# Mixer B's value products: eight matmuls of a step in one row instead of two rows of four

## The chip, the cores and the metric

The kernel runs on one core of a Trainium2 chip. The time is device microseconds of one execution of the whole program. Three runs of the kernel before gave 2955.64, 2964.18 and 2974.54 us. TensorE (PE) does the matmuls and the transposes, VectorE (DVE), ScalarE (ACT) and GpSimd (POOL) the rest; transfers are issued from SyncE (SP). PEld stands for TensorE's weight loads, which have rows of their own in the profile.

## The reference, cut to what matters

One step of a two-layer decoder for a prompt of 2048 tokens and a group of 8 samples. The even layer has two branches, A (a gated MLP) and B (stick-breaking attention with 8 heads of 64 channels); the odd layer has C (sparse attention over selected keys) and D (pooling). The change lies in B for the prompt:

```python
def stick_breaking(q, k, v, q_pos, k_pos):
    z = einsum('bqhd,bkhd->bhqk', q, k) * HEAD_DIM ** -0.5
    mask = k_pos[None, :] < q_pos[:, None]
    log_keep = where(mask, log_sigmoid(-z), 0.0)
    later = cumsum(log_keep, axis=3, reverse=True) - log_keep
    att = where(mask, exp(log_sigmoid(z) + later), 0.0)
    return einsum('bhqk,bkhd->bqhd', att, v)
```

The last line is what the value products compute. The kernel writes it with the running product `P` of the kept shares and with differences of neighbouring value rows in place of the values, so that a sum over key tiles of `P` times a tile of value differences remains.

## The kernel before, in words

The prompt's 2048 tokens are cut into four blocks of 512, and a block into four tiles of 128. `mixer_b(i)` does branch B of block i: for each of four head pairs m and each key block s from i down to 0, two steps, one for head a=0 and one for head a=1. That is 4 x (1+2+3+4) = 40 pairs of steps over the four blocks. In each pair:

- `b_logits` (one call a head): for each of four query tiles two matmuls into `z` (L839), a sigmoid on ACT (L846, or L843 with a DVE operation, L844, where mixer C's stage needs another table), on the diagonal block a mask on POOL (L849), and a scan on DVE (L853) that leaves the running product in the tile `P`.
- `b_values` (one call a head, woven with the logits of the next step): for each of four key tiles kb up to four transposes of `P` on TensorE (L876) and a copy back on ACT (L877). For head a=1 the value products follow (L885): for a key tile k, one matmul a head into the upper or the lower half of the 64-row pair in the PSUM tile `av`. They are full fp32 matmuls of 64 weight columns, and each is two records in the trace.

When s reaches 0, DVE reads `av` into `b_sum` (L892), POOL multiplies by the gate and SP stores it for the output projection.

Instructions are recorded by a Python program of generators. Each `yield` gives a cost, and `par` runs several generators side by side: it always takes the next piece from the stream that has used the smallest share of its declared cost. For mixer B the declared cost is `B(i) = 8 * (3.2 + 1.6 + 4.8 * i)`; the generator's yields come to 3.2 for the logits of two heads, 3.2 for the transposes and 1.6 after each row of value products. The order in which pieces are recorded is also the order in which tiles that share a buffer (PSUM banks above all) get it.

After recording, `Order` plans all five engines anew with a list of costs. In it matmuls on half the array's columns (`halves`) that follow each other on TensorE and write the same tile are tied into a group that stays together; the groups, and everything else, may move among each other. The result is fixed as the order of each engine's queue.

There are three stages, each with its own pools: the first does layer 0's projections and mixer B of blocks 0 to 2 (to about 1300 us in the trace), the second mixer B of block 3 beside mixer C's first tiles and the selection of keys (to about 2050 us), the third the rest of mixer C. L549 to L551 are the projections' matmuls in three parts (`pp`), L944 to L946 the output projection's (`pp_o`), L1581, L1612 and L1626 mixer C's logits, transposes and value products, L567 the samples' share of a projection, L1215 a matmul of branch D.

Of the kernel before, what the change touches and what calls it, by code (L numbers as in the profile page):

```python
# [44 lines left out]
NT = TB // P  # L45
# [393 lines left out]
class Body:  # L439
# [419 lines left out]
    def b_values(self, i, step, st, Ps):  # L859


        nc = self.nc
        m, a, s = step
        diag = s == i
        Ps = st["pT", a] = Ps[0]
        if a == 0:
            vs = st["vs"] = self.b0.tile([P, NT, P], F32, tag="vs", name="vs", bufs=self.bufs["vs"])
            nc.sync.dma_start(vs, self.vsc[s][m])
        if a and diag:
            st["av"] = self.pavb.tile([P, TB], F32, tag="av", name="av")  # L870
        vs = st["vs"]
        for kb in range(NT):
            t0, c = kb if diag else 0, slice(kb * P, (kb + 1) * P)
            pt = self.ps("ps_p", [P, NT, P])
            for t in range(t0, NT):
                nc.tensor.transpose(pt[:, t, :], Ps[:, t, c], self.idf)  # L876
            nc.scalar.copy(Ps[:, t0:, c], pt[:, t0:])  # L877
            yield 0.4
            if a == 0 or kb % 2 == 0:
                continue  # L880
            av = st["av"]
            for k in (kb - 1, kb):
                t0 = k if diag else 0
                for h in range(2):
                    nc.tensor.matmul(av[64 * h:64 * h + 64, t0 * P:], vs[:, k, 64 * h:64 * h + 64],  # L885
                                     st["pT", h][:, t0:, k * P:(k + 1) * P],
                                     start=diag and k == 0, stop=s == 0 and k == NT - 1)
            yield 1.6
        if a and s == 0:
            sm = self.tmp("b_sum")  # L890
            ve = self.vea[i][:, m].unsqueeze(2).broadcast_to([P, NT, P])
            nc.vector.tensor_tensor(sm.rearrange("p (t i) -> p t i", t=NT), st["av"].rearrange("p (t i) -> p t i", t=NT),  # L892
                                    ve, op=OP.add)
            g = self.otile("gb")
            nc.sync.dma_start(g, self.gbd[i][m])
            nc.gpsimd.tensor_tensor(sm, sm, g, op=OP.mult)
            nc.sync.dma_start(self.otd[0][i][4 + m], sm)
# [1398 lines left out]
```

## Time and profile before

| | |
|---|---|
| median of three runs | 2964.18 us |
| the profiled execution's own time | 2964.62 us |
| its span, first to last instruction | 2962.9 us |
| TensorE's granted clock, mean | 0.96 |
| busy: PE, DVE, ACT, POOL | 93%, 73%, 53%, 38% |
| idle in front of PE's z_c, longest group of waits | 27.3 us |

A busy share is an average over stages. A matmul's row gives its start and its modelled length; matmuls are pipelined, so the next one starts before the one ahead has ended, and the spacing of the starts is what a matmul takes of TensorE.

### The profile page before, as it was taken

Reading aid. Unit: us, or ns where it says so; the run is one execution under the profiler, and the core shown is the slowest. Engines: PE = TensorE matmul, PEld = TensorE weight load, DVE = VectorE, ACT = ScalarE, POOL = GpSimd, SP = SyncE. Lnnn points to the kernel's source line nnn. Section 1 sums busy time; section 2 is a strip of 40 time slices with the busy share of each in tenths; the row PEclk is TensorE's granted clock in tenths of the full one; section 3 lists DMA queues with packets and bytes.
Section 4 is the critical chain, followed back from the end, with each engine's and each line's share of the span. In section 5 each row is a group of like instructions: output and inputs, shape, how many; then the busy total and the mean of one; then the engine's idle time right before and its main releaser. Section 6 shows DMA issues by size and latency. Waiting matters only on the chain. (4 is left out here: it accounts for less than half of the span.)

```text
span 2962.9 us, 52295 instructions
## 1 busy us (share of the span) xinstructions
PE 2747.0 (93%) x17490; PEld 2184.8 (74%) x17490; DVE 2163.9 (73%) x5493; ACT 1561.7 (53%) x3148; POOL 1112.2 (38%) x1172
## 2 busy tenths in 40 slices
PE   7998999989999999979799999998899998998995
PEld 6886777767767777768477677777777887887885
DVE  2366557856775887438988998897897778887766
ACT  2433333334444344435466677784577666675852
POOL 2323335423324543242433422335422555344342
PEclk9999999999999999989899999999999999998998
DMA  7566865776585668453665455425655565675452
GB/s 220 166 175 195 266 191 186 239 227 205 172 245 165 216 184 292 147 155 111 194 173 152 140 144 146 122 79 146 189 164 157 171 190 161 213 216 172 129 185 67
DMA packets 536594, 523.51 MB, mean 177 GB/s; under 512 B 43184, under 2 KB 408905, under 8 KB 536288
## 3 DMA queue, kind: packets, MB, share of 16 engines
q1 hardware_dynamic: 526439, 484.29, 55.1%
q0 software_dynamic: 9856, 35.66, 3.9%
q8 instruction: 138, 2.26, 0.3%
q14 instruction: 161, 1.31, 0.1%
HBM read 430.27 MB, written 89.73 MB: 176 GB/s over the span
## 5 line engine op out<-in xcount | busy, mean ns | idle before, releaser
L478 POOL TENSOR_TENSOR wl<-wr,wh 128x512 fp32r<-128x512 f32 x260 | 410.7, 1580 | 967.8 <-ACT wh L475 810.5
L549 PE MATMUL pp<-xh,wh 128*128 128x512 f32 (+1 forms) x1536 | 635.6, 417 | 10.2 <-DVE q_hl L468 6.1
L550 PE MATMUL pp<-xl,wh 128*128 128x512 f32 (+1 forms) x1536 | 616.4, 402 | 9.6 <-DVE rs_t L494 8.2
L551 PE MATMUL pp<-xh,wl 128*128 128x512 f32 (+1 forms) x1536 | 616.0, 401 | 1.0 <-DVE wl L478 1.0
L475 ACT CAST wh<-wr 128x1024 fp32r<-128x1024 f32 x260 | 269.9, 1038 | 386.5 <-PE pp L550 198.7
L478 DVE TENSOR_TENSOR wl<-wr,wh 128x512 fp32r<-128x512 f32 x260 | 219.0, 843 | 210.7 <-ACT wh L475 190.0
L549 PEld LDWEIGHTS pp<-xh,wh 128*128 128x128 f32 (+1 forms) x1536 | 288.6, 189 | 95.7 <-issue 27.8
L550 PEld LDWEIGHTS pp<-xl,wh 128*128 128x128 f32 (+1 forms) x1536 | 290.6, 189 | 68.6 <-issue 9.3
L551 PEld LDWEIGHTS pp<-xh,wl 128*128 128x128 f32 (+1 forms) x1536 | 289.6, 189 | 63.9 <-issue 4.6
L944 PE MATMUL pp_o<-wh,oh 128*128 128x256 f32 x1008 | 301.0, 300 | 17.9 <-ACT oh L462 11.8
L946 PE MATMUL pp_o<-wh,ol 128*128 128x256 f32 x1008 | 291.5, 293 | 2.6 <-POOL ol L468 2.6
L945 PE MATMUL pp_o<-wl,oh 128*128 128x256 f32 x1008 | 293.2, 292 | 0.0
L853 DVE TENSOR_TENSOR_SCAN P<-P,bfst 128x512 f32<-128x512 f32 x192 | 268.5, 1408 | 22.3 <-ACT P L846 21.8
L877 ACT COPY P<-ps_p 128x512 f32<-128x512 f32 (+1 forms) x320 | 166.0, 523 | 189.2 <-PE ps_p L876 180.4
L1581 PE MATMUL z_c<-ksc,qc 128*128 128x512 f32 (+3 forms) x816 | 222.0, 355 | 32.6 <-DVE mx L1583 27.3
L1599 ACT ACTIVATE zt<-zt,nmax 128x512 f32<-128x512 f32 (+3 forms) x320 | 209.0, 655 | 76.8 <-DVE nmax L1587 76.3
L1614 ACT COPY zt<-ps_pc 128x512 f32<-128x512 f32 (+3 forms) x320 | 164.1, 520 | 114.9 <-PE ps_pc L1612 113.3
L944 PEld LDWEIGHTS pp_o<-wh,oh 128*128 128x128 f32 x1008 | 198.1, 197 | 28.7 <-ACT oh L462 13.2
L1568 POOL TENSOR_TENSOR nm<-nm,mk 128x256 f32<-128x256 f32 (+1 forms) x128 | 92.7, 725 | 335.1 <-DMA nm<-bft 186.1
L839 PE MATMUL z<-ks,q 128*128 128x512 f32 (+3 forms) x640 | 194.0, 391 | 18.9 <-DMA ks<-ksc 10.8
L946 PEld LDWEIGHTS pp_o<-wh,ol 128*128 128x128 f32 x1008 | 197.1, 197 | 8.8 <-POOL ol L468 4.5
L945 PEld LDWEIGHTS pp_o<-wl,oh 128*128 128x128 f32 x1008 | 198.5, 197 | 5.2 <-issue 2.1
(456 smaller groups left out, 5861.2 us busy)
## 6 DMA issues: line engine op xcount, KB each, us to landing
pg<-cache_b_kv SPq DMA_DIRECT2D x256, 256.0 KB
wr<-w_in_even SPq DMA_DIRECT2D x112, 512.0 KB
wr<-w_in_odd SPq DMA_DIRECT2D x76, 512.0 KB
wr<-w_out SPq DMA_DIRECT2D x68, 512.0 KB
ks<-ksc SPq DMA_DIRECT2D x80, 256.0 KB
ksc<-kcs SPq DMA_DIRECT2D x80, 256.0 KB
q<-qsc SPq DMA_DIRECT2D x64, 256.0 KB
qc<-qcs SPq DMA_DIRECT2D x128, 128.0 KB
```

The source lines that it names most:

```text
L475: nc.scalar.copy(hi, raw)
L478: e.tensor_tensor(lo[:, c], raw[:, c], hi[:, c].bitcast(F32), op=OP.subtract)
L549: nc.tensor.matmul(ps[:m], wh[:, kt, :m], xh[kt], start=a, stop=False)
L550: nc.tensor.matmul(ps[:m], wh[:, kt, :m], xl[kt], start=False, stop=False)
L551: nc.tensor.matmul(ps[:m], wl[:, kt, :m], xh[kt], start=False, stop=b)
L839: nc.tensor.matmul(z[:, :n], q2[:, c, t * P:(t + 1) * P].bitcast(F32R), ks[:, :n].bitcast(F32R), start=c == 0, stop=c == 1)
L853: nc.vector.tensor_tensor_scan(r, r, r, initial=ini, op0=OP.mult, op1=OP.bypass)
L944: nc.tensor.matmul(ps[:, :256], oh[:, tt], wh[:, k], start=a, stop=False)
L945: nc.tensor.matmul(ps[:, :256], oh[:, tt], wl[:, k], start=False, stop=False)
L946: nc.tensor.matmul(ps[:, :256], ol[:, tt], wh[:, k], start=False, stop=b)
L1581: nc.tensor.matmul(z[:, :n], q2[:, c, jj % 2, :].bitcast(F32R), kk, start=c == 0, stop=c == 1)
L1599: nc.scalar.activation(zt, zt, AF.Exp, bias=nmx, accum_out=st["rs"][:, h, c:c + 1])
```

## The change

In `b_values` the value products no longer follow every second key tile, two key tiles of two heads each; all four key tiles of both heads follow the last one. With the row that is gone goes its `yield 1.6`, so that mixer B's generator gives 8.0 instead of 9.6 for a pair of steps. `B(i)`, by which `par` shares out the stages, is as before. The matmuls themselves, their operands and their order within `av` are the same.

```diff
             yield 0.4
-            if a == 0 or kb % 2 == 0:
+            if a == 0 or kb < NT - 1:
                 continue
             av = st["av"]
-            for k in (kb - 1, kb):
+            for k in range(NT):
                 t0 = k if diag else 0
                 for h in range(2):
                     nc.tensor.matmul(av[64 * h:64 * h + 64, t0 * P:], vs[:, k, 64 * h:64 * h + 64],
                                      st["pT", h][:, t0:, k * P:(k + 1) * P],
```

TensorE's queue before, block 1, head pair 1, the diagonal key block: two rows of value products.

```order
L550 MATMUL pp<-xl,wh 128x512
L885 MATMUL av<-P,vs 64x512 x2
L885 MATMUL av<-P,vs 64x384 x2
L876 MATMUL ps_p<-idf,P 128x128 x2
L839 MATMUL z<-ks,q_6697 128x512
L876 MATMUL ps_p<-idf,P 128x128
L839 MATMUL z<-ks,q_6697 128x512 x3
L551 MATMUL pp<-xh,wl 128x512
L885 MATMUL av<-P,vs 64x256 x2
L885 MATMUL av<-P,vs 64x128 x2
L839 MATMUL z<-ks,q_7261 128x128 x2
```

TensorE's queue after, the same pair of steps:

```order
L551 MATMUL pp<-xh,wl 128x512
L885 MATMUL av<-P,vs 64x512 x2
L885 MATMUL av<-P,vs 64x384 x2
L885 MATMUL av<-P,vs 64x256 x2
L885 MATMUL av<-P,vs 64x128 x2
L876 MATMUL ps_p<-idf,P 128x128 x4
L549 MATMUL pp<-xh,wh 128x512
```

The eight matmuls stand together, and the transposes and logits that stood between them stand outside.

TensorE's queue before, near the end of mixer B of block 3, at the first row of its last pair of steps (the second follows 16 rows below it; `zt` and `ksc` are mixer C's):

```order
L567 MATMUL ps_smp<-wl,xsT 16x128
L885 MATMUL av<-P,vs 64x512 x4
L1612 MATMUL ps_pc<-idf,zt 128x128 x4
L876 MATMUL ps_p<-idf,P 128x128 x4
L1215 MATMUL ps_m<-pl,dwg 128x512
L551 MATMUL pp<-xh,wl 128x512
L1581 MATMUL z_c<-ksc,qc 128x512 x2
```

TensorE's queue after, the same last value products of block 3:

```order
L551 MATMUL pp<-xh,wl 128x512
L885 MATMUL av<-P,vs 64x512 x8
L1271 MATMUL z_i<-kid,qi 128x512
L567 MATMUL ps_smp<-wh,xsT 16x128
L1612 MATMUL ps_pc<-idf,zt 128x128 x4
```

Of the four `ps_m` matmuls of that block three stand ahead of the last value products before (the `ps_m` row above is the third), and none after: all of mixer B of block 3 has moved ahead of them. In PE's queue as a whole, 80 rows of four `av` matmuls have become 40 of eight, and the last of them stands some 410 matmuls earlier among 15336.

## Rows read from the trace of the kernel before

**Rows 1.** The page: span, and busy time of each engine.

```profile
span 2962.9 us, 52295 instructions
PE 2747.0 (93%) x17490; PEld 2184.8 (74%) x17490; DVE 2163.9 (73%) x5493; ACT 1561.7 (53%) x3148; POOL 1112.2 (38%) x1172
```

**Rows 2.** Busy time by stretch: PE, PEld, DVE, ACT, POOL, granted clock, DMA share, GB/s.

```profile
60.00:129.00 69.00, 69.00 (x438) 57.07 (x437) 19.52 (x41) 26.06 (x44) 20.36 (x13) 1.00 0.60 172
190.00:460.00 270.00, 260.75 (x1344) 197.62 (x1344) 151.26 (x310) 93.16 (x178) 90.81 (x99) 0.98 0.69 208
460.00:520.00 60.00, 53.92 (x354) 46.18 (x355) 44.08 (x52) 24.05 (x45) 36.27 (x39) 0.91 0.57 178
520.00:1290.00 770.00, 746.63 (x3986) 561.05 (x3985) 531.61 (x795) 317.94 (x580) 275.18 (x277) 0.99 0.67 205
1290.00:1345.00 55.00, 38.65 (x231) 33.07 (x232) 28.07 (x57) 24.13 (x52) 29.47 (x33) 0.84 0.58 167
1345.00:1690.00 345.00, 310.95 (x1853) 232.21 (x1850) 298.61 (x890) 199.72 (x445) 128.07 (x149) 0.95 0.55 154
1690.00:2005.00 315.00, 306.42 (x2069) 228.41 (x2068) 279.69 (x887) 241.60 (x521) 91.43 (x124) 0.99 0.45 126
```

**Rows 3.** The tile `av`: its matmuls, shortest, median and longest in ns.

```profile
L885 PE MATMUL av<-P,vs x640: 272/592/1117, 179.9 to 2004.7; 128*64 128x512 f32 x112, 128*64 128x384 f32 x16, 128*64 128x256 f32 x16, 128*64 128x128 f32 x16
```

**Rows 4.** Timeline of PE, a full row among projections: start us, length us.

```profile
640.73 0.39 PE L551 MATMUL pp<-xh,wl 128*128 128x512 f32 x1
...
642.09 0.39 PE L551 MATMUL pp<-xh,wl 128*128 128x512 f32 x1
642.41 1.94 PE L885 MATMUL av<-P,vs 128*64 128x512 f32 x8
644.28 0.50 PE L549 MATMUL pp<-xh,wh 128*128 128x512 f32 x1
644.62 0.40 PE L550 MATMUL pp<-xl,wh 128*128 128x512 f32 x1
```

**Rows 5.** Timeline of PE, a short row (key tiles 2 and 3, diagonal).

```profile
382.49 0.39 PE L551 MATMUL pp<-xh,wl 128*128 128x512 f32 x1
382.81 0.87 PE L885 MATMUL av<-P,vs 128*64 128x256 f32 x8
383.61 0.50 PE L549 MATMUL pp<-xh,wh 128*128 128x512 f32 x1
383.95 0.40 PE L550 MATMUL pp<-xl,wh 128*128 128x512 f32 x1
```

**Rows 6.** Timeline of PE, a full row among output projections.

```profile
1023.06 0.28 PE L946 MATMUL pp_o<-wh,ol 128*128 128x256 f32 x1
1023.27 1.94 PE L885 MATMUL av<-P,vs 128*64 128x512 f32 x8
1025.13 0.39 PE L944 MATMUL pp_o<-wh,oh 128*128 128x256 f32 x1
1025.36 0.28 PE L945 MATMUL pp_o<-wl,oh 128*128 128x256 f32 x1
1025.48 0.28 PE L946 MATMUL pp_o<-wh,ol 128*128 128x256 f32 x1
```

**Rows 7.** Waits of PE from 1345 to 2005 us: total us, times, longest.

```profile
PE z_c L1581 <- DVE mx L1583: 9.4, 5, 5.1
PE z L839 <- DVE mx L1583: 4.6, 5, 1.6
```

**Rows 8.** Groups of DVE instructions from 1345 to 2005 us, mixer B's.

```profile
L853 DVE TENSOR_TENSOR_SCAN P<-P,bfst 128x512 f32<-128x512 f32 x95 | 123.7, 1304 | 0.2
L844 DVE TENSOR_SCALAR P<-P 128x512 f32<-128x512 f32 (+1 forms) x119 | 53.5, 451 | 9.4 <-ACT P L843 8.5
```

**Rows 9.** Waits of PE from 1290 to 1345 us: total us, times, longest.

```profile
PE pp_o L944 <- ACT oh L462: 10.3, 2, 8.9
```

**Rows 10.** Timeline of PE, the last row of block 2's value products.

```profile
1251.78 1.94 PE L885 MATMUL av<-P,vs 128*64 128x512 f32 x8
```

## The prediction

> **What bounds the kernel now.** I read the page's first part, then the table by stretch, then the waits of TensorE. The page shows TensorE busy for 2747 of 2962.9 us [rows 1]. The table by stretch [rows 2] tells where this is a real limit. From 190 to 460 us it is busy for 260.75 of 270 us, from 520 to 1290 for 746.63 of 770, from 1690 to 2005 for 306.42 of 315. These are the stretches in which mixer B runs: its value products start at 179.9 us and end at 2004.7 [rows 3]. The places where TensorE lacks work are the changes between phases: 460 to 520 us (6.1 us idle, granted clock 0.91) and 1290 to 1345 (16.4 us idle, clock 0.84). From 1345 to 1690 it is busy for 311 of 345 us, with DVE at 299; even there and to 2005 us only 14.0 us of its waiting is put down to DVE in the two largest groups [rows 7]. So for most of the time until 2005 us the next matmul is ready when the one ahead is done, and what a matmul takes of TensorE is what it costs the kernel. The end, from 2005 us on, holds no mixer B and stands in almost the same order in both programs, so I leave it alone.
>
> **What a row of value products costs beside its work.** The length of a matmul in the timeline is modelled, so I go by spacings of starts. Among projections [rows 4] the matmuls start 0.227 us apart ((642.09 - 640.73) / 6, the rows between them left out). The full row of eight records starts there 0.32 us after the matmul ahead of it instead of 0.23; the next projection comes at 644.28, and the one after that 0.34 us later instead of 0.23. From the matmul ahead (642.09) to the second matmul behind (644.62) it is 2.53 us; two ordinary spacings are 0.45, so the row costs 2.08 us. The short row [rows 5] (256 and 128 columns instead of 512 and 512) takes 383.95 - 382.49 = 1.46 us, less 0.45 is 1.01. Both have eight records. Summed over them the columns are 4096 against 1536 (4 x 512 + 4 x 512, and 4 x 256 + 4 x 128), so 1.07 us pays for 2560 columns: 0.42 ns a column, and 1.71 us for the full row. What is left, 2.08 - 1.71 = **0.37 us**, doesn't depend on the columns: it is the price of coming from whole-array matmuls to half-array matmuls and back. Among output projections [rows 6] the same sum goes 1025.36 - 1023.06 = 2.30, less two spacings of 0.12, less 1.71: 0.35 us. The two agree, though the neighbours differ.
>
> The Trainium skill has a price for this: the page TensorEngine Tiling (Array Packing), section Key Properties, says that changing the tiling mode drains the engine, and TensorE: Matmul & The Clock Gate, section Step-by-step: what each phase is for, gives a drain of about 128 cycles, 53 ns at 2.4 GHz. By it, as an estimate, 40 rows fewer with two changes each would give back 4.3 us, and the time would be 2960. The rows above show three to four times as much for a change there and back, so the measurement decides, and the sum goes by 0.37.
>
> **The change part by part.**
>
> *Forty row edges removed.* There are 80 rows of four matmuls before, none next to another, and 40 of eight after. The work stays the same. 40 x 0.37 = 14.8 us; at 0.35 it is 14.0. Of these, 24 lie in the first stage (blocks 0 to 2: 4 + 8 + 12 pairs of steps), 8.9 us, where TensorE is the limit; 16 lie in the second, 5.9 us. In its first half TensorE has 34 us of idle time in 345, so part of what is saved may turn into waiting. I let it lose up to half there: 12 to 15 us are gained in all, and I take **13**.
>
> *The row waits for the fourth copy.* The first four products could start after the second copy of `P` (L877), now all eight wait for the fourth. Behind them in TensorE's queue stand projections and logits. In the planned order other work is put between the last transposes and the row, as the order shows, and the last four products waited for that copy already. `P` and `vs` were held until the second row's end, and it comes up to half a row's work, 1.7 us, later after the last copy. Cover: the projections, which need neither. I count nothing; were it not covered, 1.7 us x 16 pairs in the second stage, where there are only three `P` buffers, would be 27 us of DVE's waiting, of which TensorE would feel what it can't fill.
>
> *TensorE is taken for 3.7 us in one piece* instead of twice 2.1 us. Whoever waits for a `z` in that time waits 1.6 us longer. DVE and ACT are not the limit in the first stage (DVE 151 of 270 us, 532 of 770). Nothing counted there.
>
> *Mixer B is recorded earlier.* This is the part that the text of the change hides. A pair of steps yields 8.0 instead of 9.6 units, while the declared sum stays. So `par` takes mixer B's pieces faster, and its stream ends at 83% of its phase. The planned order shows it: the last row of block 3 stands some 410 matmuls earlier, which is about 73 us at the rate of the trace, those of block 0 up to 60, block 2 up to 55. Total work is unchanged; it is denser first, and then projections and mixer C go on alone. Projections alone keep TensorE full: from 60 to 129 us, before mixer B begins, it is busy for 69.0 of 69 us [rows 2]. So in the first stage I expect nothing inside the phases. At their changes mixer B might be missing as filling, or might be done before it is needed. The nearest rows, 460 to 520 us, bound this: 6.1 us idle plus 60 x 0.09 = 5.4 us for the clock, 11.5 us, to either side. I take zero.
>
> Sum: 2964.6 - 13 = **2952 us**. The profiled execution's own time is 2964.62 us, 1.7 us above its span, and lies 0.4 us from the median of the runs. That is 0.4%, and the three runs lie 0.6% apart; a measurement of this kernel can hardly tell less than 1% from no change.
>
> **The rivals.**
>
> *No change.* The edges are saved, but at one change of phase more TensorE waits, since mixer B, which filled it, is through: 2964.6 - 13 + 11.5 = 2963. For it speaks that from 460 us on, block 0's last transposes and products stood among the projections, and that they are now 60 us ahead. Against it: block 1's logits come there too, and the gap exists already with mixer B near.
>
> *Slower: DVE becomes the limit in the second stage.* From 1345 to 2005 us DVE is busy for 578 of 660 us, 88%. Mixer B's share is some 199 us: 123.7 for the scans of full tiles and 53.5 for L844 [rows 8] and about 22 for the diagonal's scans. If mixer B ends 75 us earlier, DVE has to do 199 + 379 x 585/660 = 535 us of work in 585, which is 91%. If it can't go above 88%, that takes 610 us, and mixer B's matmuls come 25 us late. If TensorE can fill none of it, the time is 2964.6 - 13 + 25 = 2977 us; with a lower clock after the waits some 15 us more. It decides from the point where TensorE's waits for DVE in this stage, now 14 us, grow by more than the 13 saved. Against it: TensorE has projections to fill with, and waits for DVE at all for only 2% of that time.
>
> *Faster by more.* Mixer B's earlier end lets the next output projection start without its wait. The largest is at 1290 to 1345 us: 16.4 us idle, of which 10.3 wait for the split of its input [rows 9], and 55 x 0.16 = 9 us for the clock. Without it the time is 2964.6 - 13 - 25 = 2927 us. Against it: mixer B of block 2 starts its last row at 1251.8 us [rows 10], some 40 us ahead of that wait, so it is hardly what was waited for.
>
> *The change doesn't do what it says* can be left out: the eight stand together in the planned order in all 40 places.
>
> **How the numbers follow.** 2952 within 6 us: 0.48. No change, 2958 to 2968: 0.24. Slower, 2968 to 3000: 0.17, of which the part above 2994 (1%) is 0.09. Faster by more, 2925 to 2946: 0.11, which I let count as below 2935, with a little of the forecast's own tail, 0.13 in all. That leaves 0.78 within 1%. The range leaves out the outer half of both outer cases: 2930 to 2986.
>
> **What would show it.** Rows of `av` in the timeline with sixteen records, about 3.8 us from the matmul ahead to the second one behind less two spacings (2 x 1.71 + 0.37), in 40 places; TensorE's busy time down by some 13 us with the same instructions, DVE's, ACT's and POOL's as before. The last `av` matmul near 1925 us instead of 2004.7. The stretch up to the third stage shorter by about 13 us, and the rest as long as before. I am wrong if TensorE's idle time at the changes of phase, or its waits for DVE behind 1345 us, move by more than 13 us, for then the order of the plan decides and not the edges.

## The result, and the profile after

The changed kernel takes 2984.01 us (median of 9 runs, 2975.65 to 2996.34), the kernel before in the same runs 2965.26 us (median of 9): a ratio of 1.0073, 95% interval 1.0055 to 1.0091. It is some 19 us slower, where 13 us faster was forecast. The time lies inside the range; the sign is wrong.

The page after, span and busy time; [rows 1] are its counterpart:

```profile
span 2982.3 us, 52316 instructions
PE 2741.7 (92%) x17490; PEld 2191.9 (73%) x17490; DVE 2180.5 (73%) x5493; ACT 1559.9 (52%) x3148; POOL 1119.8 (38%) x1172
```

TensorE is busy for 5.3 us less than before, in a span that is 19.4 us longer. So the time in which it is not busy (span less busy) rose from 215.9 to 240.6 us, by 24.7. A matmul's end is modelled, so these two numbers are good for comparing kernels and no more. The mean granted clock is 0.956 instead of 0.960; at that clock the same work takes longer. The clock missing from full speed is 0.044 x 2982.3 = 131 us instead of 0.040 x 2962.9 = 119, so up to some 13 us of longer matmuls can be put down to it (an estimate); that is enough for the 9.5 us by which TensorE's busy time fell short of the forecast's 14.8, but the edges' share of it can't be read from this one pair of traces.

The timeline of PE after, one of the 24 full rows, among projections (as [rows 4]):

```profile
864.59 0.39 PE L550 MATMUL pp<-xl,wh 128*128 128x512 f32 x1
864.81 0.40 PE L551 MATMUL pp<-xh,wl 128*128 128x512 f32 x1
865.14 3.65 PE L885 MATMUL av<-P,vs 128*64 128x512 f32 x16
868.72 0.50 PE L549 MATMUL pp<-xh,wh 128*128 128x512 f32 x1
869.07 0.40 PE L550 MATMUL pp<-xl,wh 128*128 128x512 f32 x1
```

From the matmul ahead to the second one behind it is 869.07 - 864.81 = 4.26 us; less two spacings (0.46) it is 3.80, which is the forecast's number, and less 8192 columns (3.42) it leaves 0.38 us. One of the 16 rows on the diagonal (5120 columns), and a full row among output projections, as [rows 5] and [rows 6]:

```profile
345.87 0.39 PE L551 MATMUL pp<-xh,wl 128*128 128x512 f32 x1
346.18 2.38 PE L885 MATMUL av<-P,vs 128*64 128x512 f32 x16
348.49 0.50 PE L549 MATMUL pp<-xh,wh 128*128 128x512 f32 x1
348.82 0.40 PE L550 MATMUL pp<-xl,wh 128*128 128x512 f32 x1
...
1378.14 0.28 PE L946 MATMUL pp_o<-wh,ol 128*128 128x256 f32 x1
1378.35 3.65 PE L885 MATMUL av<-P,vs 128*64 128x512 f32 x16
1381.93 0.39 PE L944 MATMUL pp_o<-wh,oh 128*128 128x256 f32 x1
1382.15 0.28 PE L945 MATMUL pp_o<-wl,oh 128*128 128x256 f32 x1
```

They leave 2.95 - 0.46 - 2.13 = 0.36 us and 4.01 - 0.24 - 3.42 = 0.35. The price of an edge is what the prediction read before, whatever the row's length and neighbours; there are 40 rows of 16 records now. The same sum over every row that stands among projections or output projections at the full clock and without a gap gives 0.35 to 0.37 us for 23 rows before and 0.36 to 0.38 us for 15 after.

The table by stretch after (columns as in [rows 2]):

```profile
190.00:460.00 270.00, 257.28 (x1346) 196.28 (x1345) 149.16 (x303) 92.48 (x176) 89.38 (x97) 0.97 0.70 207
460.00:520.00 60.00, 54.28 (x354) 47.38 (x353) 50.58 (x64) 25.27 (x48) 41.39 (x42) 0.97 0.67 197
520.00:1290.00 770.00, 742.85 (x4007) 566.58 (x4005) 525.97 (x791) 316.39 (x578) 279.72 (x275) 0.98 0.67 204
1290.00:1345.00 55.00, 39.97 (x235) 34.06 (x234) 28.05 (x58) 23.84 (x52) 29.85 (x32) 0.84 0.58 165
1345.00:1690.00 345.00, 314.29 (x1855) 237.37 (x1855) 301.22 (x865) 197.88 (x434) 119.30 (x141) 0.93 0.52 151
1690.00:2005.00 315.00, 297.03 (x1982) 219.50 (x1980) 273.12 (x849) 228.19 (x503) 92.24 (x125) 0.97 0.45 127
```

The changes of phase, on which the forecast had set its bound, did not move: from 460 to 520 us TensorE is busy for 54.28 instead of 53.92 us at a better clock, from 1290 to 1345 for 39.97 instead of 38.65. TensorE is busy less inside the phases: from 520 to 1290 us it lacks 3.8 us more than before, from 1690 to 2005 us 9.4 us more, with the clock two hundredths lower. Matmul by matmul, by the place where each stands in the kernel before, the gaps ahead of them grew by 8.2 us up to 1290 us, fell by 1.9 from there to 1690, and grew by 7.8 to 2005 and by 10.0 behind 2005 us, where there is no mixer B at all.

Mixer C's first logits open the second stage. Their matmuls before and after (shortest, median, longest in ns; first and last start in us):

```profile
L1581 PE MATMUL z_c<-ksc,qc x816: 220/364/797, 1329.2 to 2914.6; 128*128 128x512 f32 x65, 128*128 128x256 f32 x58, 128*128 128x128 f32 x35, 128*128 128x384 f32 x6
L1581 PE MATMUL z_c<-ksc,qc x816: 218/364/794, 1330.4 to 2933.4; 128*128 128x512 f32 x65, 128*128 128x256 f32 x58, 128*128 128x128 f32 x35, 128*128 128x384 f32 x6
```

The first comes 1.2 us later than before, the last 18.8 us: the first stage lost what its 24 rows should have gained, and nearly all of the lag arose behind it.

The waits of PE after that name a place, in three views (0 to 1297 us, 1345 to 2005 us, and from 2060 us; total, times, longest):

```profile
PE ps_sa L1801 <- DVE s_sgm L1798: 7.6, 1, 7.6
...
PE ps_su L1795 <- POOL s_tr L1792: 6.2, 3, 4.0
...
PE ps_x L525 <- DMA xc<-x: 13.7, 4, 10.6
PE z_c L1581 <- DVE mx L1583: 9.0, 10, 1.5
PE z_i L1271 <- DVE mx L1583: 5.7, 3, 4.1
...
PE ps_sc L1977 <- DVE s_c L1986: 6.9, 1, 6.9
```

`ps_sa`, `ps_su` and `ps_sc` belong to the samples' small branches, `ps_x` to the load of a projection's input. In the kernel before there is no wait of `ps_sa` for `s_sgm` nor of `ps_sc` for `s_c L1986`, and `ps_su` waits for 1.0 us in all. None of these matmuls is part of the change. The largest single waits are the load's, which ends at 1454.6 us (10.6 us in one piece; before 3.9), and the samples', which end at 1116.6 (7.6) and 2152.4 us (6.9).

DVE's groups of mixer B from 1345 to 2005 us (the scans against [rows 8]; L844 has two shapes in one row there, so its full tiles stand here before and after), and the tile `av`, against [rows 3]:

```profile
L853 DVE TENSOR_TENSOR_SCAN P<-P,bfst 128x512 f32<-128x512 f32 x95 | 126.0, 1329 | 0.1
L844 DVE TENSOR_SCALAR P<-P 128x512 f32<-128x512 f32 x101 | 46.5, 462 | 7.8 <-ACT P L843 7.5
L844 DVE TENSOR_SCALAR P<-P 128x512 f32<-128x512 f32 x101 | 51.5, 511 | 4.9 <-ACT P L843 4.7
```

```profile
L885 PE MATMUL av<-P,vs x640: 272/592/1117, 193.8 to 1952.1; 128*64 128x512 f32 x112, 128*64 128x384 f32 x16, 128*64 128x256 f32 x16, 128*64 128x128 f32 x16
```

The last value product starts 52.6 us earlier than before.

### The profile page after: what moved, and what is told of

It is laid out like the page before. It is cut to its first block, busy times and chain, and to the rows that moved or that the text cites. A ratio compares the mean times of both kernels' runs of the same rounds, so it can differ in the third digit from the quotient of the medians.

```text
span 2982.3 us, 52316 instructions
## 1 busy us (share of the span) xinstructions
PE 2741.7 (92%) x17490; PEld 2191.9 (73%) x17490; DVE 2180.5 (73%) x5493; ACT 1559.9 (52%) x3148; POOL 1119.8 (38%) x1172
## 5 line engine op out<-in xcount | busy, mean ns | idle before, releaser
L853 DVE TENSOR_TENSOR_SCAN P<-P,bfst 128x512 f32<-128x512 f32 x192 | 266.0, 1394 | 21.7 <-ACT P L846 21.4
L1327 ACT ACTIVATE mk<-ix,tk_tn 128x512 int8<-128x512 f32 (+13 forms) x140 | 183.4, 1310 | 31.7 <-DVE tk_tn L1377 20.5
```

What stands on the lines that cost most here:

```text
L853: nc.vector.tensor_tensor_scan(r, r, r, initial=ini, op0=OP.mult, op1=OP.bypass)
```

## The experiments

Two words first. **The plan** is the order of all five queues that the planner makes out of its list of costs. **A draw** of it is what the planner makes when one of those costs, `SEM` (what it counts for a signal from one engine to another, 150), is set to 146, 148, 152 or 154. That changes the order, not the work: each engine has the same number of instructions in every page (PE 17490, DVE 5493, ACT 3148, POOL 1172). Ratios are to the kernel before in the runs of the same chip (median 2962 to 2964 us).

### Was it the faster pace of mixer B's stream?

The changed kernel with the pace of the kernel before (one row, 3.2 units behind it), the kernel before with the pace of the changed one (two rows, 0.8 each), and one row with the old pace in block 3 only:

```diff
# e1_paced, against the changed kernel
-            yield 1.6
+            yield 3.2
# e2_two_rows_early, against the kernel before
-            yield 1.6
+            yield 0.8
# e3_paced_block3, against the changed kernel
-            yield 1.6
+            yield 3.2 if i == NB - 1 else 1.6
```

> The changed kernel, but the one row of eight is followed by a yield of 3.2 instead of 1.6, so that mixer B's stream gives 9.6 a pair of steps as before and keeps its pace. Theory 1 (the pace: the lost 1.6 units let mixer B run ahead of mixer C in the second stage, which then ends late): about 2951 us, 13 below the kernel before, since the 40 edges are saved; the last av matmul near 2000 us again. Theory 2 (the long row: 3.7 us in one piece that waits for four copies starves DVE and ACT): about 2984, as the changed kernel. Theory 3 (any new plan moves the time by 20 us for no reason of its own): anything from 2945 to 2985.

> The kernel before with its two rows of four, but a yield of 0.8 after each instead of 1.6: 8.0 a pair of steps, the pace of the changed kernel without its long rows. Theory 1: slower than the changed kernel by the edges, about 2984 + 13 = 2997 us, with the last av matmul near 1930 us. Theory 2: about 2965, as the kernel before. Theory 3: anything from 2950 to 2990.

> The changed kernel with the yield of 3.2 in block 3 alone (the second stage), 1.6 in blocks 0 to 2. Theory 1 with the loss in the second stage: within 6 us of the kernel that is paced throughout, about 2951 to 2960 us. If the early pace costs in the first stage too, 2965 or more. Theory 2: about 2984.

Measured: one row at the old pace 2961.14 us, 1.0002 [0.9984, 1.0020]; two rows at the new pace 2990.53, 1.0108 [1.0091, 1.0125]; old pace in block 3 alone 2975.8, 1.0059 [1.0036, 1.0083]. Taken alone, these three say that the pace costs 23 to 28 us and that the row is worth nothing or 7 us. Theory 2 (2984, 2965 and 2984) is out by 23 and 26 us in the first two. None comes out at theory 1's first numbers either (2951, 2997, 2951 to 2960); the third fits only its addition that the pace costs in the first stage too. And each of them is a new plan as well, which had no control yet.

### What does a new plan cost by itself?

```diff
# c1_before_sem, against the kernel before (c2_before_148: 148)
-    SEM, DMA_START, DMA_END, RATE = 150, 700, 1500, 280.0
+    SEM, DMA_START, DMA_END, RATE = 152, 700, 1500, 280.0
```

> The kernel before with one number of the planner's cost list changed (a semaphore's delay of 152 instead of 150 ns), so that the plan is drawn anew, nothing else. Theories 1 and 2: within 6 us of the kernel before, 2959 to 2971. Theory 3: it moves by 10 us or more, to either side.

> The kernel before, planned with a semaphore delay of 148 ns: a third draw of its plan. Theory 3 (the plan of the kernel before is a lucky one, and any new plan costs some 10 to 25 us): 2975 to 2990, and the loss lies again behind 1300 us. If 152 was the odd one out: 2959 to 2971.

Measured: 2984.36 us at 152, 1.0090 [1.0056, 1.0123], and 2982.47 at 148, 1.0066 [1.0048, 1.0084]. Only theory 3 allowed for this: the kernel before, with the same two rows, the same pace and the same instructions, becomes as slow as the changed kernel in both of these new plans. How far a new plan reaches can be counted in the traces: of TensorE's 17490 matmuls, some 2600 have another matmul ahead of them than before, in either plan. In the changed kernel it is some 2900. The edit of 40 rows has redrawn the plan as thoroughly as a changed cost does.

### One row in the old plan

Here no planner runs: the order of every queue is read from a table, that of the kernel before, in which only the first row of each pair has been moved down TensorE's queue to the second (`e6_moved_sem`: the same with the plan of `c1_before_sem`). In the traces 120 matmuls of 17490 have another one ahead of them.

```diff
# e5_moved, against the kernel before
-            yield 0.4
-            if a == 0 or kb % 2 == 0:
+            yield from (0.4, 1.6) if a and kb == 1 else (0.4,)
+            if a == 0 or kb < NT - 1:
...
-            for k in (kb - 1, kb):
+            for k in range(NT):
...
-        order.gather()
-        order.settle()
+        order.order = unpack()
```

> The value products of a step in one row as in the change, but not planned anew: every engine's queue is that of the kernel before, word for word, only the first row of four of each of the 40 steps is moved down TensorE's queue to stand directly ahead of the second. Theory 1 (edges are saved; the changed kernel lost by its plan, by pace or by chance): 12 to 15 us under the kernel before, about 2950 us. Theory 2 (the long row itself, 3.7 us in one piece behind the fourth copy, starves others): 2965 or more, up to the changed kernel's 2984.

> The same done to the plan of the kernel before that was drawn with the semaphore delay of 152 ns (2984 us): 40 rows moved together, all else as there. Theory 1: 12 to 15 us under that one, about 2970 us. Theory 2: 2984 or more.

Measured: 2983.24 us, 1.0068 [1.0051, 1.0084], and 2997.46, 1.0102 [1.0066, 1.0138]. The first is slower than the plan that it was made from, though 40 edges are gone and nothing else has moved. The second is 13 us above its own by the medians, but four runs of each, with ratios of 1.0102 and 1.0090, don't tell it from that plan; it isn't faster by 12 to 15 us, as theory 1 had it. I went through the traces of `e5_moved` and of the kernel before matmul by matmul (the sequences are the same but for the rows). The value products and the matmul behind each row take 12.5 us less, as the edges have it. Against that TensorE stands idle for 13.1 us more, matmuls that now come behind a gap or no longer do are 5.2 us longer in sum, and those that run at another level of the clock than before, 2.4 or 1.2 GHz, take 8.4 us more; 1.2 us are spread over the rest: 13.1 + 5.2 + 8.4 + 1.2 - 12.5 = 15.4 us of the 16.4 by which the spans differ. The idle time is firm; the other parts shift by a few us with the kind under which a matmul that fits two of them is counted. Where the idle time comes from, in the waits of PE of `e5_moved` from 190 to 460 and from 520 to 1290 us:

```profile
PE ps_sz L1776 <- DVE s_z L1770: 3.0, 1, 3.0
...
PE ps_su L1795 <- POOL s_tr L1792: 4.4, 3, 2.2
PE pp L549 <- DVE q_hl L468: 3.4, 2, 1.9
PE ps_x L525 <- DVE xl L468: 3.1, 2, 3.0
PE ps_sav L1809 <- DMA pg<-cache_b_kv: 2.7, 4, 1.8
```

The same waits in the kernel before are none, 1.0, 1.9, 2.5 and 1.4 us. A row that is moved down takes its 2 us out of the place where it stood; what stood behind it there is reached sooner, and its inputs, made by DVE, POOL and transfers, are not there yet. The plan had set them apart for a TensorE that has a row in between.

The numbers of `e5_moved` are also those of theory 2, by which the long row starves the others. The place of the new idle time tells the two apart. Ahead of the matmuls that stand between the two rows of a pair, which are now reached sooner, it grew by 21.7 us. Ahead of the next 30 matmuls behind each long row it fell by 1.5 us, and elsewhere by 7.1. In `e6_moved_sem`, against `c1_before_sem`, it is 24.1, -1.5 and -5.0 us. So the new idle time lies in the hole that a row leaves, and not behind the long row.

### Draws of the changed kernel, and of one row at the old pace

> One row of eight with the pace kept (a yield of 3.2), planned with 148 ns: a second draw of the paced kernel, which gave 2961. By theory 3 together with saved edges: 2955 to 2980, some 13 us under the two-row kernel's mean over its new draws. By theory 1 alone with no chance in the plan: 2961 again within 6 us.

> One row of eight with 3.2 units behind it (the pace of two rows kept), planner's cost of a semaphore at 152. Theory 1: 2984 (two rows, the same draw) - 14 = 2970, from 2962 to 2978, below the changed kernel in the same draw. Theory 2: about the middle of the draws so far, 2980, with 10 us to either side, and no order to the changed kernel of the same draw.

> The changed kernel with the planner's cost of a semaphore at 148 instead of 150, which only draws the plan anew. Theory 1 (the edges give back about 14 us, the faster pace of mixer B's stream costs about as much, and every draw of the plan scatters by some 10 us about that): as its siblings of the same draw stand at 2982 (two rows) and 2972 (one row, old pace), it comes to 2982 - 14 + 15 = 2983, from 2975 to 2992, and above its sibling with the old pace. Theory 2 (only the draw of the plan matters, edges and pace nothing that can be told): anywhere from 2960 to 2995, and as likely below the sibling as above it.

> The changed kernel with the planner's cost of a semaphore at 152. Theory 1: its sibling with two rows stands at 2984, so 2984 - 14 + 15 = 2985, from 2975 to 2995, and 10 to 15 us above the one with one row and the old pace that is run beside it. Theory 2: anywhere from 2960 to 2995, without an order between the two.

Measured: one row at the old pace 2971.92 us at 148, 1.0023 [1.0001, 1.0045], and 2966.37 at 152, 1.0012 [0.9996, 1.0028]; the changed kernel 2956.18 at 148, 0.9970 [0.9954, 0.9987], and 2966.79 at 152, 1.0011 [0.9995, 1.0028]. With the faster pace I had looked for 2983 and 2985. Theory 1 as written falls in its second half: the changed kernel is 16 us below its sibling of the old pace at 148, level with it at 152, and 23 us above it at 150. A cost of the pace can't be told. The same code as in the result, with another number in the planner's list, is 28 us faster than the changed kernel and 7.5 us faster than the kernel before.

The waits of that fastest plan (`e8_after_148`, PE, 0 to 1297 us, 1297 to 2060 us, and from 2060 us) warn against taking the large waits after for the cause:

```profile
PE ps_sa L1801 <- DVE s_sgm L1798: 7.6, 1, 7.6
...
PE ps_su L1795 <- POOL s_tr L1792: 5.8, 2, 4.2
...
PE ps_x L525 <- DMA xc<-x: 10.1, 3, 7.3
...
PE ps_sc L1977 <- DVE s_c L1986: 6.3, 1, 6.3
```

The three new waits of the samples are here too, nearly as long as in the result. All waits of TensorE together come to 191 us in this plan and to 208 us in the result: it is the sum of many that differs.

### Two further draws of both kernels

> The kernel before with the planner's cost of a semaphore at 146: a fourth draw of its plan. Theory 1 (the rows' edges are worth about 14 us, and a draw scatters by some 12 us about that): three draws stand at 2977 on average, so 2977 with 12 us to either side, and above the changed kernel of the same draw. Theory 2 (only the draw): the mean of all six draws of the two kernels, 2973, with 12 us to either side, and no order between the two. Theory 3 (150 was a favourable draw for the kernel before): above 2964.

> The changed kernel, semaphore at 146. Theory 1: 2977 - 14 = 2963, with 12 us to either side, below the kernel before of the same draw. Theory 2: 2973 with 12 us to either side. Theory 3 (150 was an unfavourable draw for the changed kernel): below 2984.

> The kernel before, semaphore at 154. The same numbers as at 146: theory 1 2977 and above the changed kernel of the same draw, theory 2 2973 without an order, theory 3 above 2964.

> The changed kernel, semaphore at 154. The same numbers as at 146: theory 1 2963 and below the kernel before of the same draw, theory 2 2973 without an order, theory 3 below 2984. Over the five draws of each, theory 1 has the changed kernel some 10 us lower on average, theory 2 within 5 us.

Measured: at 146 the kernel before 2992.77 us, 1.0110 [1.0090, 1.0131], the changed one 2975.69, 1.0054 [1.0036, 1.0071]; at 154 the kernel before 2958.34, 0.9986 [0.9967, 1.0004], the changed one 2969.21, 1.0021 [1.0009, 1.0034]. Theory 3 misses at 154 for the kernel before (2958, not above 2964). Both times of the kernel before, 2993 and 2958, lie outside the 12 us that theories 1 and 2 allowed, and the order that theory 1 asked for holds at 146 and not at 154. Neither of the two is decided by the medians, as the table shows: time is the median of the runs, the other columns are of the profiled execution (busy from its page, not busy is span less busy).

| `SEM` | two rows: time | busy | not busy | one row: time | busy | not busy |
|---|---|---|---|---|---|---|
| 146 | 2992.8 | 2765.8 | 225.2 | 2975.7 | 2741.5 | 232.7 |
| 148 | 2982.5 | 2750.7 | 226.2 | 2956.2 | 2732.5 | 222.7 |
| 150 | 2965.3 | 2747.0 | 215.9 | 2984.0 | 2741.7 | 240.6 |
| 152 | 2984.4 | 2755.4 | 230.0 | 2966.8 | 2730.1 | 229.2 |
| 154 | 2958.3 | 2745.4 | 218.2 | 2969.2 | 2741.4 | 226.0 |
| mean | 2976.6 | 2752.9 | 223.1 | 2970.4 | 2737.4 | 230.2 |

The pages of the two kernels at 146 and of the fastest, from which three lines of the table are:

```profile
span 2991.0 us, 52285 instructions
PE 2765.8 (92%) x17490; PEld 2190.1 (73%) x17490; DVE 2174.9 (73%) x5493; ACT 1562.5 (52%) x3148; POOL 1115.9 (37%) x1172
```

```profile
span 2974.2 us, 52310 instructions
PE 2741.5 (92%) x17490; PEld 2191.2 (74%) x17490; DVE 2175.2 (73%) x5493; ACT 1558.9 (52%) x3148; POOL 1124.7 (38%) x1172
```

```profile
span 2955.2 us, 52304 instructions
PE 2732.5 (92%) x17490; PEld 2185.8 (74%) x17490; DVE 2171.5 (73%) x5493; ACT 1562.4 (53%) x3148; POOL 1122.6 (38%) x1172
```

Three things are to be seen. Busy: all five plans with two rows lie at 2745 us or above, all five with one row at 2742 or below, and the means differ by 15.4 us, with mean clocks of 0.959 in both (0.957 to 0.962, and 0.956 to 0.963). The three plans at the old pace with one row agree (2732.5 to 2740.9), and so do `e2_two_rows_early` (2749.1) and `e3_paced_block3` (2735.3). The difference of the means has an error of 4 us, so it agrees with the forecast's 14.8 us. The two kernels with rows moved in a foreign plan, 2749.4 and 2747.8 (7.6 below the plan that it was made from), are the exception; for the first, the count above says why. Not busy: it scatters by 14 to 18 us within each kernel, and its mean is 7.1 us higher with one row. Time: the means differ by 6.2 us in favour of the change, but within a kernel the draws scatter by 14 and 10 us (standard deviation), so the error of that difference is sqrt(14.2²/5 + 10.3²/5) = 8 us. The pairs of one draw go -17, -26, +19, -18 and +11. The time thus settles neither theory 1 (some 10 us) nor theory 2 (within 5 us).

One mark inside the program, chosen after the fact, shows the row's worth better. The first `z_c` matmul starts, from 146 to 154, at 1346.1, 1331.7, 1329.2, 1338.7 and 1323.6 us with two rows, and at 1322.2, 1318.2, 1330.4, 1318.0 and 1318.0 us with one. The means differ by 12.5 us, with an error of 5, where the 24 rows of the first stage should give 8.9. From the first `z_c` to the last, one row then takes 4.6 us more on average, with an error of 3.5, where the other 16 rows should have saved 5.9.

## Why the prediction was wrong

*What bounds the kernel, and the edge's price: right.* 0.35 to 0.38 us in three kinds of row, and over five plans TensorE is busy for 15.4 us less, where 14.8 was worked out. The Trainium skill's page TensorEngine Tiling (Array Packing), section Key Properties, says only that a change of the tiling mode drains the engine; the 4.3 us that the prediction estimated from it and a drain's length for the same 40 rows are not what these runs show.

*The row waits for the fourth copy: nothing, right as far as shown.* DVE's scans in the second stage had 0.2 us of idle time ahead of them and have 0.1. ACT, which writes `P` there (L843), waited for the value products (L885) for 3.0 us in that stretch and does not wait for them now. The bad case of 27 us did not come.

*TensorE taken for 3.7 us in one piece: nothing named.* TensorE's own waits for a free `z` behind ACT's sigmoid (`P` L846, 0 to 1297 us) rose from 1.1 to 5.0 us, but they are 7.2 and 3.7 us in the two redraws of the kernel before at 152 and 148, and 1.7 in the changed kernel at 148: they go with the draw, not with the length of a row.

*Mixer B is recorded earlier, "I take zero": this is the step that failed, and "I leave it alone" for the end, from 2005 us on, failed with it.* It looked at one effect of the new order, that mixer B's filling might be missing where phases change, and bounded it by the idle time there, 11.5 us. The phases' changes did not move. What moved was the rest: about one matmul in six stands behind another one than before, and TensorE's time without work rose by 24.7 us, much of it ahead of matmuls that have nothing to do with mixer B: 10 us of it behind 2005 us. There some 400 of 6600 matmuls have another one ahead of them, which is little, but not nothing. The stretch up to the third stage, forecast 13 us shorter, is about 13 us longer: the matmuls that stand from 2030 to 2060 us before come 12.5 us later (median). The condition that I had named for being wrong, as it was written, is not met: TensorE's waits at the changes of phase went from 5.9 to 5.6 us and from 16.1 to 14.7, its waits for DVE behind 1345 us from 82.5 to 85.8. The idle time moved elsewhere, and the order of the plan decided all the same. A bound was to be had from this kernel only by drawing its plan anew: five draws of the kernel before span 34 us, five of the changed one 28.

That the time lies in the range all the same is luck: the range went up to 2986 for the sake of a rival that did not come.

*The kernel before as the base.* The sum was made against one plan, 2964.6 us, as if the change kept it. That plan is the second best of five, whose mean is 2977 us. Draw 150 stands 11 us below the mean of the kernel before and 14 us above that of the changed one. The means themselves differ by 6 us the other way: 11 + 14 - 6 = 19 us is the result.

*The rivals.* DVE as the limit in the second stage, which came out nearest to the time (2977), was not the way: DVE is busy for 574.3 us from 1345 to 2005, where it was 578.3, and its largest waits in that stretch hardly grew (`z_c`, `z` and `z_i` for `mx`: 9.0 + 1.5 + 5.7 = 16.2 us, where it was 9.4 + 4.6 + 0.7 = 14.7). The last `av` matmul came at 1952 us, not near 1925, so mixer B was not pressed together as far as assumed either.

*My first explanation after the result fell as well.* Three runs pointed to a cost of the pace; two draws of the changed kernel undid it.

What stays open: whether one row is worth anything in time on average over the whole program. The busy time says 15 us, the first stage alone 12.5, the time without work gives about 7 back (argued from five plans of each, with an error of 4 us), and the median of a plan says what the draw makes of it. I have not tried a planner that is told of the saved edge.

The best version that was run is the changed kernel with the planner's cost of a signal at 148: 2956.18 us, 0.9970 [0.9954, 0.9987] of the kernel before. It is the best of 17 plans, and so owes something to being picked.

## What to carry to other kernels

Where a planner sets the order, an edit is measured together with a redraw of the whole plan; draw both kernels' plans a few times, by a small change of one cost, before crediting or blaming the edit, and take the scatter (here 10 to 14 us, 0.4%) into the range of a forecast. Busy time of the bounding engine tells a saved piece of work from a lucky order: on the mean of five plans it fell by what the rows said (by 4 to 25 us in the pairs of one draw), while the time did not follow. A piece that is taken out of a tight order leaves a hole that the other engines can't fill sooner, so moving it by hand without a new plan can cost more than it saves. What comes behind the part that is changed is in the plan as well: a forecast that leaves it alone needs a reason.

## What the runs showed of the hardware that was not expected

The price of an edge between whole-array and half-array matmuls is one number: 0.38, 0.36 and 0.35 us there and back, for rows of 5120 and 8192 columns as before for 1536 and 4096, among projections and output projections. And more gaps came with longer matmuls: in the plan with the rows moved, 13.1 us of added idle time stood beside 13.6 us of longer matmuls, 8.4 of them on matmuls that ran at another of the two clock levels than before. The granted clock was lower in its other runs too, with a median of 0.9575 over 10 runs against 0.962 over 25 of the kernel before on the same chip. That the gaps lowered the clock is not shown: no run changes the one without the other.
